# First projection of a hybrid encoder layer: finished blocks in two 512-column buffers, six weight quadrants held, loads into the buffer freed last

## Chip, cores and metric

The kernel runs on one core of a Trainium2 chip. The metric is the device time of one execution in microseconds (us). Before the change three runs gave 2162.06, 2162.21 and 2162.73 us; their median is 2162.21 us. Engines are named as the profile names them: PE multiplies matrices, PEld loads its weights, ACT and DVE work on whole tiles, POOL and SP here mostly issue DMA transfers.

## What is computed

One encoder layer over 512 tokens of width 2048, in float32:

```
h = rmsnorm(x, attn_norm_w)
proj = h @ w_in
aq, ak, av, gq, gk, gv, gr, glr = split(proj)
...
x = x + concat([attn_out, gla_out]) @ w_out
h = rmsnorm(x, ffn_norm_w)
x = x + (silu(h @ w_gate) * (h @ w_up)) @ w_down
return rmsnorm(x, final_norm_w)
```

The change lies in `proj = h @ w_in`, in those 4096 columns of it that are called gr, gq, gk, aq and ak.

## The kernel before

**Units and steps.** The class `Front` computes these columns in 16 units of 256 columns by 512 tokens: four of gr, four of gq and gk, eight of aq and ak. A unit is a two-by-two block product done with seven products instead of eight: weights and activations are both cut into quadrants, sums of quadrants are formed on DVE, and seven products are added up in accumulators of PSUM called X, V, Y, W and Z. One product is a *step*, numbered n = 0 to 6 in its unit (and i over all 112). `Feed` computes w_gate and w_up with the same step code (both inherit from `Units`).

**What one step costs.** Every float32 operand is split into a high and a low part. ACT casts the weight quadrant to the high part (`cast`, L1563), DVE subtracts to get the low part (`sub`, L1569), and DVE adds quadrants where the product wants a sum (`add`, L1538). PE then does eight matmuls of 128 x 512 with the high part (L1601) and eight of 128 x 256 with the low part (L1604).

**Order of the work.** `Front.run` goes over the steps. In loop step i it first asks for weight loads (`fetch`, issued by SP, L1531), then emits cast, add and sub of step i + 2 (`lead`), then empties what step i - 1 left in PSUM (`evac_`), and last emits the matmuls of step i. Each engine works through its own part in this order. Where a step reads an accumulator that `evac_` has to read first, PE waits: product 6 adds to W, which the add at L1645 (emptying step 4) reads.

**Emptying.** After n = 0, 1 and 2 ACT copies accumulators (L1629, L1632, L1636) and DVE subtracts (L1638). After n = 3, 5 and 6 ACT copies (L1623) and DVE adds (L1624) a quarter of the finished block; after n = 4 DVE adds at L1645 and L1647. Then `finish` scales the block on DVE (L1801, or L1799 for two units) and POOL writes it to DRAM (L1802).

**Buffers.** `s4` is a pool of 33 buffers of 128 x 1024, named b0 to b32; `s2` has 36 of 128 x 512, named a0 to a35. `get` takes the buffer that has been free longest, `put` appends one at the end. A buffer is put back when the program has emitted its last reader, which may be well before that reader runs: whoever gets the buffer waits for it. Weight quadrants, sums of quadrants, high parts, low parts and the finished block all come from `s4`. `fetch` holds up to eight quadrants and leaves at least three buffers free (`KEEP`). `sub` puts its source back, `products` the high and low part, and `finish` the finished block, whose last reader is the write to DRAM.

Quadrant tiles are 128 x 8 x 128, 512 KB. The following lines show the mechanism:

```
s.i = self.free.popleft()
...
hi, lo = self.his.pop(i), s4.get(F32R, [P, NP, P])
...
if n == 3:
    self.outs[u] = s4.get(F32, [P, 2, 512])
    out("X", 0)
```

Of the kernel before, what the change touches and what calls it, by code (L numbers as in the profile page):

```python
# [19 lines left out]
OP = mybir.AluOpType  # L20
# [94 lines left out]
def put(*slots):  # L115
    for s in slots:
        if s.home is not None:
            s.home.free.append(s.i)


def layer(nc, tc, x, attn_norm_w, w_in, rel_table, gw_f, gb_f, gw_b, gb_b, gla_norm_w, w_out,
# [7 lines left out]
    with tc.manual_schedule(), \  # L129
# [1381 lines left out]
        class Units:  # L1511

            ORDER = ("B11", "T1", "T2", "B21", "T3", "B22", "T4")
            FREES = {0: "B11", 4: "T3", 5: "B22", 6: "T4"}
            AHEAD, KEEP = 2, 3

            def open(self, first):
                self.steps = [(u, n) for u in range(first, len(self.units)) for n in range(7)]
# [5 lines left out]
            def fetch(self, most=8):  # L1524
                while self.todo and len(self.quads) < most and len(s4.free) > self.KEEP:
                    u, b = self.todo.popleft()
                    r = self.quads[u, b] = s4.get(F32, [P, NP, P])
                    w, col = self.place(u)
                    k, h = divmod(b, 2)
                    rows = w[:, col + h * P:col + (h + 1) * P].rearrange("(q k p) c -> k p q c", k=2, p=P)  # L1530
                    sp.dma_start(out=r.t, in_=rows[k])  # L1531
# [77 lines left out]
            def evac_late(self):  # L1609
                late, self.late_ = self.late_, []  # L1610
                for i in late:
                    self.evac_(i)

            def evac_(self, i):

                u, n = self.steps[i]
                B = lambda k: self.banks[u, k]
                a, z = slice(0, 256), slice(256, 512)
                tt = dve.tensor_tensor

                def out(k, c):
                    o = self.outs[u].t.rearrange("p f t -> p (f t)")[:, c * 256:(c + 1) * 256]
                    act.copy(o, B(k).t[:, a])  # L1623
                    tt(o, o, B(k).t[:, z], op=OP.add)  # L1624
                    put(self.banks.pop((u, k)))

                if n == 0:
                    b = self.banks[u, "Y"] = self.seat(i + 1)
                    act.activation(b.t, B("X").t, AF.Copy, scale=-1.0)  # L1629
                if n == 1:  # L1630
                    y = self.parts[u] = s2.get()
                    act.copy(y.t, B("V").t)  # L1632
                    put(self.banks.pop((u, "V")))
                if n == 2:
                    b = self.banks[u, "W"] = self.seat(i + 1)
                    act.activation(b.t, B("Y").t, AF.Copy, scale=-1.0)  # L1636
                    b = self.banks[u, "Z"] = self.seat(i + 1)
                    tt(b.t, self.parts[u].t, B("Y").t, op=OP.subtract)  # L1638
                    put(self.banks.pop((u, "Y")))
                if n == 3:  # L1640
                    self.outs[u] = s4.get(F32, [P, 2, 512])
                    out("X", 0)
                if n == 4:
                    y = self.parts.pop(u)
                    tt(y.t, y.t, B("W").t, op=OP.add)  # L1645
                    o = self.outs[u].t.rearrange("p f t -> p (f t)")
                    tt(o[:, 768:1024], y.t[:, a], y.t[:, z], op=OP.add)  # L1647
                    put(y)
                if n == 5:
                    out("Z", 1)  # L1650
                if n == 6:
                    out("W", 2)
                    c_ = self.outs.pop(u)
                    urgent.append(self.finish(u, c_, c_.t.rearrange("p f t -> p (f t)")))

        class Feed(Blocks, Units):

# [40 lines left out]
            def evac(self, u, banks):  # L1698


                a, z = slice(0, 256), slice(256, 512)
                w, j = self.units[u]
                add = lambda o, x_, y_: dve.tensor_tensor(o, x_, y_, op=OP.add)
                c_ = s4.get(F32, [P, 2, 512])
                c = c_.t.rearrange("p f t -> p (f t)")
                A, B, C, E = (b.t for b in banks)
                t1, t2 = s2.get(), s2.get()
                act.copy(t1.t[:, a], A[:, a])
                add(c[:, a], A[:, z], t1.t[:, a])
# [11 lines left out]
                yield from self.finish(u, c_, c)  # L1721
                yield

            def finish(self, u, c_, c):
                w, j = self.units[u]
                if w is w_gate:
                    dve.tensor_tensor(c_.t, c_.t, rb[2].t[:, None, :].to_broadcast([P, 2, 512]), op=OP.mult)
                    yield
                    tables(SILU)
                    for f in range(2):  # L1730
                        act.activation(c_.t[:, f], c_.t[:, f], AF.Silu, scale=1.0 - 2.0 * f)
                    self.gate = c_
                else:
                    dve.tensor_tensor(c_.t, c_.t, self.gate.t, op=OP.mult)
                    put(self.gate)
                    pool.dma_start(out=gd[j], in_=c)
                    put(c_)

            def run(self):
# [42 lines left out]

        class Front(Units):

            def __init__(self):
                self.units = [(w_in, C_GR + g * 256) for g in range(4)] + [(w_in, C_GQ), (w_in, C_GK)] + \
                    [(w_in, C_GQ + 256), (w_in, C_GK + 256)] + \
                    [(w_in, c + g * 256) for g in range(4) for c in (C_AQ, C_AK)]
                self.xs = xi
                self.open(0)  # L1790
# [1 line left out]
            def place(self, u):  # L1792
                return self.units[u]

            def finish(self, u, c_, c):
                def do():
                    r = rb[1].t[:, None, :].to_broadcast([P, 2, 512])
                    if u in (4, 6):
                        dve.scalar_tensor_tensor(c_.t, c_.t, P ** -0.5, r, op0=OP.mult, op1=OP.mult)  # L1799
                    else:  # L1800
                        dve.tensor_tensor(c_.t, c_.t, r, op=OP.mult)  # L1801
                    pool.dma_start(out=grd[u] if u < 4 else gfd[u - 4] if u < 8 else qkd[u - 8], in_=c)  # L1802
# [571 lines left out]
```

## Time and profile before

| what | value |
|---|---|
| median of three runs | 2162.21 us |
| the profiled execution, its own time | 2165.34 us |
| its span in the trace | 2163.6 us |
| PE busy | 2135.8 us (99%), 11418 matmuls |
| DVE busy | 1724.6 us (80%) |
| ACT busy | 1229.1 us (57%) |
| steps of `Front` in the trace | 106.3 us to 441.8 us |
| steps of `Feed` in the trace | about 896 us to 1718 us |

The profiled execution took 3.1 us more than the median of the runs; its own time is 1.7 us more than its span. A view called *waits* names, for each group of instructions, whom it waited for, the total in us, the number of times and the longest. In a *timeline* a row has its start, its length, the engine, the line and the operation, merged over a few instructions (x8), and in brackets how long the engine had been idle before it and who ended that. In a table *by windows* each engine has its busy time in that stretch, and PEclk is the granted TensorE clock. Lengths of matmuls overlap, so a step's length is best read from starts.

### The profile page before, as it was taken

To read this page: it belongs to the slowest core of one execution; us is meant where nothing else is said; L and a number is where in the kernel's file an instruction comes from. 1 tells how busy PE (TensorE), PEld (TensorE's weight loads), DVE (VectorE), ACT (ScalarE), POOL (GpSimd) and SP (SyncE) were. 2 spreads that over 40 slices of the span, in tenths; PEclk is the share of its full clock that TensorE was granted. 3 is DMA by queue.
4 is the path that set the end of the run, shared out by engine and by line. 5 is a ranking of instruction groups with operands and counts; after the bars stand their busy time and mean duration, and the time that the engine had idled before them with its cause. 6 is when DMAs were issued, how large, how long until landed. Compare 5 with 4: busy or idle time off the path is not lost.

```text
span 2163.6 us, 30507 instructions
## 1 busy us (share of the span) xinstructions
PE 2135.8 (99%) x11418; PEld 1835.3 (85%) x11418; DVE 1724.6 (80%) x2345; ACT 1229.1 (57%) x2051; POOL 172.6 (8%) x278
## 2 busy tenths in 40 slices
PE   9999999999999999999999999999999999999998
PEld 7887888888888888988888888888888888888887
DVE  5677787868877657988888888888888878897885
ACT  7444444457786545555545555555555576666762
POOL 0000000112312000000000000000000020232000
PEclk9999999999999999999999999999999999999999
DMA  6543444365754423444434334443344497899572
GB/s 203 172 149 108 136 120 134 105 199 171 201 199 140 134 98 117 137 127 123 116 113 136 116 118 117 127 132 112 114 130 117 173 241 248 200 256 241 194 256 78
DMA packets 340594, 330.47 MB, mean 153 GB/s; under 512 B 15133, under 2 KB 260365, under 8 KB 340446
## 3 DMA queue, kind: packets, MB, share of 16 engines
q1 hardware_dynamic: 313598, 258.07, 39.1%
q0 software_dynamic: 26528, 69.91, 12.5%
q8 instruction: 90, 1.47, 0.3%
q14 instruction: 58, 0.48, 0.1%
q10 hardware_dynamic: 320, 0.53, 0.1%
HBM read 267.55 MB, written 60.92 MB: 152 GB/s over the span
## 4 chain that ended last, share of the span: by engine, by line
PE 83%; issue 13%; DMA 1%; DVE 1%; ACT 1%; POOL 0%; DVEq 0%; SPq 0%; POOLq 0%; ACTq 0%
PE ps L1601 26%; PE ps L1604 14%; PE ps L349 6%; PE ps L350 6%; PE ps L348 6%; PE ps L2057 5%; PE ps L2056 5%; PE ps L2055 5%; PE ps L699 1%; PE ps L2270 1%; PE ps L2272 1%; PE ps L2271 1%; PE ps L643 1%; PE ps L724 1%; PE ps L723 1%
## 5 line engine op out<-in xcount | busy, mean ns | idle before, releaser
L1569 DVE TENSOR_TENSOR b<-b,b 128x1024 fp32r<-128x1024 f32 x406 | 495.2, 1220 | 133.9 <-ACT b L1563 122.0
L1563 ACT CAST b<-b 128x1024 fp32r<-128x1024 f32 x406 | 425.9, 1050 | 200.7 <-DVE b L1569 92.0
L1601 PE MATMUL ps<-a,b 128*128 128x512 f32 x1656 | 427.0, 393 | 16.4 <-DVE a L1645 11.1
L1601 PE MATMUL ps<-b,b 128*128 128x512 f32 x1592 | 421.2, 393 | 0.5 <-ACT ps L1629 0.5
L1601 PEld LDWEIGHTS ps<-a,b 128*128 128x128 f32 x1656 | 304.8, 189 | 81.9 <-issue 13.2
L1601 PEld LDWEIGHTS ps<-b,b 128*128 128x128 f32 x1592 | 280.2, 189 | 43.2 <-ACT ps L1629 0.7
L1538 DVE TENSOR_TENSOR b<-b,b 128x1024 f32<-128x1024 f32 x232 | 282.6, 1218 | 1.3 <-PE ps L350 0.7
L1604 PEld LDWEIGHTS ps<-b,b 128*128 128x128 f32 x1592 | 232.6, 190 | 23.4
L1604 PE MATMUL ps<-a,b 128*128 128x256 f32 x1656 | 242.9, 283 | 0.0
L1604 PE MATMUL ps<-b,b 128*128 128x256 f32 x1592 | 242.8, 282 | 0.0
L1604 PEld LDWEIGHTS ps<-a,b 128*128 128x128 f32 x1656 | 225.2, 192 | 8.5
L1623 ACT COPY b<-ps 128x256 f32<-128x256 f32 x174 | 64.6, 371 | 223.5 <-PE ps L1604 223.5
L2031 DVE TENSOR_TENSOR b<-b,b 128x1024 fp32r<-128x1024 f32 x112 | 136.5, 1220 | 34.8 <-ACT b L2023 34.8
L348 PE MATMUL ps<-b,b 128*128 128x512 f32 x344 | 139.8, 407 | 0.0
L350 PE MATMUL ps<-b,b 128*128 128x512 f32 x344 | 135.1, 393 | 0.0
L349 PE MATMUL ps<-b,b 128*128 128x512 f32 x344 | 134.9, 392 | 0.0
L2023 ACT CAST b<-b 128x1024 fp32r<-128x1024 f32 x112 | 116.6, 1052 | 26.6 <-DVE b L2011 15.3
L220 DVE TENSOR_TENSOR b<-b,b 128x512 fp32r<-128x512 f32 x120 | 79.5, 683 | 26.7 <-ACT b L239 26.5
L1624 DVE TENSOR_TENSOR b<-b,ps 128x256 f32<-128x256 f32 x174 | 72.2, 415 | 27.7 <-ACT b L1623 27.7
L2055 PE MATMUL ps<-b,a 128*128 128x512 f32 x240 | 93.4, 389 | 0.0
L2056 PE MATMUL ps<-b,a 128*128 128x512 f32 x240 | 93.4, 389 | 0.0
L2057 PE MATMUL ps<-b,a 128*128 128x512 f32 x240 | 93.4, 389 | 0.0
(308 smaller groups left out, 3580.6 us busy)
## 6 DMA issues: line engine op xcount, KB each, us to landing
b<-in_w_in_dram SPq DMA_DIRECT2D x94, 512.0 KB, 4.1
b<-in_w_gate_dram SPq DMA_DIRECT2D x88, 512.0 KB, 4.4
b<-in_w_up_dram SPq DMA_DIRECT2D x88, 512.0 KB, 3.8
b<-in_w_down_dram SPq DMA_DIRECT2D x88, 512.0 KB, 6.9
b<-in_w_out_dram SPq DMA_DIRECT2D x32, 512.0 KB, 4.4
md<-a POOLq DMA_DIRECT2D x56, 256.0 KB, 6.8
gd<-b POOLq DMA_DIRECT2D x22, 512.0 KB, 5.3
b<-gd SPq DMA_DIRECT2D x22, 512.0 KB, 5.5
```

What stands on the lines that cost most here:

```text
L348: mm(o, xh.t[:, c], wh.t[:, w], start=first and not on, stop=False, skip_group_check=on)
L349: mm(o, xh.t[:, c], wl.t[:, w], start=False, stop=False, skip_group_check=on)
L350: mm(o, xl.t[:, c], wh.t[:, w], start=False, stop=last, skip_group_check=on)
L1538: tt = lambda o, x_, y_: dve.tensor_tensor(o.t, x_.t, y_.t, op=OP.add)
L1563: act.copy(hi.t, home[key].t)
L1569: dve.tensor_tensor(lo.t, home[key].t, hi.f, op=OP.subtract)
L1601: mm(o.rearrange("p (s t) -> p s t", s=2), hi.t[:, q], self.xs[q][self.ORDER[n]], start=new and q == 0, stop=False, skip_group_check=True)
L1604: mm(o[:, 0:256], lo.t[:, q], self.xs[q][self.ORDER[n]][:, 0], start=False, stop=q == NP - 1, skip_group_check=True)
L2031: dve.tensor_tensor(lo.t, s.t, hi.f, op=OP.subtract)
L2055: mm(o, xh[:, t], wh, start=new and j == 0, stop=False, skip_group_check=True)
L2056: mm(o, xh[:, t], wl, start=False, stop=False, skip_group_check=True)
L2057: mm(o, xl[:, t], wh, start=False, stop=last and j == 1, skip_group_check=True)
```

## The change

Four things change, all in this one stage; one of them touches code that `Feed` uses too, without effect there.

- The finished block of `Front` is held in two `s2` buffers of 128 x 512 (`home`, `block`) instead of one `s4` buffer.
- `finish` therefore scales it with two instructions of 128 x 512 and writes it with two transfers of 256 KB.
- `Front` holds six weight quadrants instead of eight: `fetch(6)`. The loads asked for before the stage begins still go up to eight.
- In `Front` a load takes the `s4` buffer that was put back last, instead of the one free longest (`NEWEST`, a rotation of the list of free buffers). All others still take the oldest.

```
@@ class Units
+            NEWEST = False
             def fetch(self, most=8):
                 while self.todo and len(self.quads) < most and len(s4.free) > self.KEEP:
                     u, b = self.todo.popleft()
+                    if self.NEWEST:
+                        s4.free.rotate(1)
                     r = self.quads[u, b] = s4.get(F32, [P, NP, P])
...
+            def home(self):
+                return s4.get(F32, [P, 2, 512])
+
+            def block(self, u, c):
+                return self.outs[u].t.rearrange("p f t -> p (f t)")[:, c * 256:(c + 1) * 256]
...
                 if n == 3:
-                    self.outs[u] = s4.get(F32, [P, 2, 512])
+                    self.outs[u] = self.home()
                     out("X", 0)
@@ class Front(Units)
+            NEWEST = True
+
+            def home(self):
+                return s2.get(), s2.get()
+
+            def block(self, u, c):
+                f, h = divmod(c, 2)
+                return self.outs[u][f].t[:, h * 256:(h + 1) * 256]
+
-            def finish(self, u, c_, c):
+            def finish(self, u, c_):
                 def do():
-                    r = rb[1].t[:, None, :].to_broadcast([P, 2, 512])
-                    if u in (4, 6):
-                        dve.scalar_tensor_tensor(c_.t, c_.t, P ** -0.5, r, op0=OP.mult, op1=OP.mult)
-                    else:
-                        dve.tensor_tensor(c_.t, c_.t, r, op=OP.mult)
-                    pool.dma_start(out=grd[u] if u < 4 else gfd[u - 4] if u < 8 else qkd[u - 8], in_=c)
-                    put(c_)
+                    d = grd[u] if u < 4 else gfd[u - 4] if u < 8 else qkd[u - 8]
+                    for f, o in enumerate(c_):
+                        if u in (4, 6):
+                            dve.scalar_tensor_tensor(o.t, o.t, P ** -0.5, rb[1].t, op0=OP.mult, op1=OP.mult)
+                        else:
+                            dve.tensor_tensor(o.t, o.t, rb[1].t, op=OP.mult)
+                        pool.dma_start(out=d[:, f * 512:(f + 1) * 512], in_=o.t)
+                    put(*c_)
...
                 for i, (u, n) in enumerate(self.steps):
-                    self.fetch()
+                    self.fetch(6)
                     self.lead(i + self.AHEAD)
```

PE's instructions stay in the same order. What moves is which buffer each of the others gets. In the rows below a tile's name begins with its buffer: b32_239 is a tile in buffer b32, the number behind it only counts tiles. All are from the end of unit 5 and the beginning of unit 6.

ACT before, from the last quarter of unit 5's block (b32_227, which is later scaled and written to DRAM) to the fourth cast after it:

```order
L1623 COPY b32_227_2064<-ps3_61_2038 128x256
L1563 CAST b16_237_2159<-b30_209_1931 128x1024
L1629 ACTIVATE ps6_64_2163<-ps5_63_2138 128x512
L1563 CAST b32_239_2182<-b18_199_1855 128x1024
L1632 COPY a8_66_2187<-ps7_65_2165 128x512
L1563 CAST b18_243_2209<-b5_232_2110 128x1024
L1636 ACTIVATE ps0_66_2213<-ps6_64_2163 128x512
L1563 CAST b8_245_2233<-b26_194_1807 128x1024
```

The second cast goes into b32, the buffer of the block that is just being written to DRAM, and the third into b18, the very buffer that the second has read. ACT at the same place after the change:

```order
L1632 COPY a9_77_2076<-ps3_61_2049 128x256
L1566 CAST b19_229_2173<-b9_213_2041 128x1024
L1638 ACTIVATE ps6_64_2177<-ps5_63_2152 128x512
L1566 CAST b28_231_2196<-b14_200_1917 128x1024
L1641 COPY a10_78_2201<-ps7_65_2179 128x512
L1566 CAST b29_235_2223<-b6_225_2124 128x1024
L1645 ACTIVATE ps0_66_2227<-ps6_64_2177 128x512
L1566 CAST b30_237_2247<-b10_194_1865 128x1024
```

The block is in a8 and a9, and none of the four casts goes into a buffer named in the rows before it.

DVE before, at the same place: the last quarter of the block, its scaling (L1801), and the subs of the next casts:

```order
L1569 TENSOR_TENSOR b8_235_2134<-b5_232_2110,b9_234_2132 128x1024
L1624 TENSOR_TENSOR b32_227_2064<-b32_227_2064,ps3_61_2038 128x256
L1801 TENSOR_TENSOR b32_227_2064<-b32_227_2064,a28_45_650 128x1024
L1569 TENSOR_TENSOR b6_238_2161<-b30_209_1931,b16_237_2159 128x1024
L1538 TENSOR_TENSOR b5_232_2110<-b5_232_2110,b30_209_1931 128x1024
L1569 TENSOR_TENSOR b19_240_2185<-b18_199_1855,b32_239_2182 128x1024
```

DVE there after the change, where the scaling is L1819:

```order
L1572 TENSOR_TENSOR b17_228_2148<-b6_225_2124,b12_227_2146 128x1024
L1633 TENSOR_TENSOR a9_77_2076<-a9_77_2076,ps3_61_2049 128x256
L1819 TENSOR_TENSOR a8_76_2075<-a8_76_2075,a28_45_650 128x512
L1819 TENSOR_TENSOR a9_77_2076<-a9_77_2076,a28_45_650 128x512
L1572 TENSOR_TENSOR b26_230_2175<-b9_213_2041,b19_229_2173 128x1024
L1541 TENSOR_TENSOR b6_225_2124<-b6_225_2124,b9_213_2041 128x1024
L1572 TENSOR_TENSOR b22_232_2199<-b14_200_1917,b28_231_2196 128x1024
```

One instruction has become two, at the same place in the row; everything else stands as it stood, with other buffers.

SP before, the four quadrants of unit 6 and the first of unit 7:

```order
L1531 DMA b26_194_1807<-in_w_in_dram 128x8x128
L1531 DMA b18_199_1855<-in_w_in_dram 128x8x128
L1531 DMA b19_200_1857<-in_w_in_dram 128x8x128
L1531 DMA b30_209_1931<-in_w_in_dram 128x8x128
L1531 DMA b17_215_1982<-in_w_in_dram 128x8x128
```

SP after, the same five loads:

```order
L1534 DMA b10_194_1865<-in_w_in_dram 128x8x128
L1534 DMA b14_200_1917<-in_w_in_dram 128x8x128
L1534 DMA b12_203_1942<-in_w_in_dram 128x8x128
L1534 DMA b9_213_2041<-in_w_in_dram 128x8x128
L1534 DMA b32_214_2043<-in_w_in_dram 128x8x128
```

The loads stand in the same order, but each is asked for later in the program: the fourth of unit 6 at loop step n = 3 of unit 5, where it stood at n = 6 of unit 4 before; the fifth in the same loop step as the fourth, where it stood at n = 1 of unit 5. Their buffers, b9 and b32, are those of the low and the high part of unit 5's product n = 2, the product that PE does just before.

More of the change, by code (lines that the diff above doesn't have):

```diff
@@ L1621, in out @@
                 def out(k, c):
-                    o = self.outs[u].t.rearrange("p f t -> p (f t)")[:, c * 256:(c + 1) * 256]
+                    o = self.block(u, c)
                     act.copy(o, B(k).t[:, a])
@@ L1645, in evac_ @@
                     tt(y.t, y.t, B("W").t, op=OP.add)
-                    o = self.outs[u].t.rearrange("p f t -> p (f t)")
-                    tt(o[:, 768:1024], y.t[:, a], y.t[:, z], op=OP.add)
+                    tt(self.block(u, 3), y.t[:, a], y.t[:, z], op=OP.add)
                     put(y)
@@ L1735, in finish @@
                     put(self.gate)
-                    pool.dma_start(out=gd[j], in_=c)
+                    pool.dma_start(out=gd[j], in_=c_.t.rearrange("p f t -> p (f t)"))
                     put(c_)
```

6 lines of the change are left out of this document (3 added, 3 removed).

## The prediction

> **What bounds the kernel now.** I read the page first: PE fills 99% of the span. So only what shortens or opens PE's pauses counts, and the next question is where they are. The table by windows answers that (columns PE, PEld, DVE, ACT, POOL, then PEclk):
>
> ```profile
> PE 2135.8 (99%) x11418; PEld 1835.3 (85%) x11418; DVE 1724.6 (80%) x2345; ACT 1229.1 (57%) x2051; POOL 172.6 (8%) x278
> ...
> 200.00:300.00 100.00, 94.13 (x532) 81.84 (x531) 78.54 (x86) 46.11 (x63) 2.12 (x4) 1.00 0.44 122
> 300.00:400.00 100.00, 94.98 (x540) 82.72 (x539) 79.54 (x87) 45.83 (x62) 2.66 (x5) 1.00 0.46 132
> 1000.00:1400.00 400.00, 400.00 (x2292) 351.98 (x2291) 340.40 (x368) 209.28 (x289) 5.31 (x10) 1.00 0.42 122
> ```
>
> In `Front` PE stands still for over 5 us in each 100. In `Feed` (1000 to 1400), with the same step code, it never does, although DVE has more to do there (85% against 79%). So `Front` does not lack engine time; it waits in the wrong places. PE's own waits, whole program:
>
> ```profile
> PE ps L1601 <- DVE a L1645: 11.1, 12, 1.1
> PE ps L1601 <- ACT ps L1629: 4.0, 2, 3.5
> PE ps L1601 <- ACT ps L1636: 1.7, 2, 1.4
> ```
>
> Twelve times, once per unit, product 6 waits for the add at L1645. The third row is two more waits in these units. Next I read the timeline at one such wait, the one that ends unit 6; POOL's row is the write of unit 5's block, on which the chain begins:
>
> ```profile
> 240.56 0.53 POOL L1802 DMA_DIRECT2D gfd<-b  x1 [20.09 <-DVE b L1801]
> 243.53 1.05 ACT L1563 CAST b<-b 128x1024 fp32r<-128x1024 f32 x1 [3.33 <-DMA gfd<-b]
> 244.61 1.22 DVE L1569 TENSOR_TENSOR b<-b,b 128x1024 fp32r<-128x1024 f32 x1 [2.07 <-ACT b L1563]
> 245.87 1.05 ACT L1563 CAST b<-b 128x1024 fp32r<-128x1024 f32 x1 [0.81 <-DVE b L1569]
> 246.95 1.23 DVE L1569 TENSOR_TENSOR b<-b,b 128x1024 fp32r<-128x1024 f32 x1 [1.12 <-ACT b L1563]
> ...
> 250.59 2.00 PE L1601 MATMUL ps<-b,b 128*128 128x512 f32 x8
> 253.57 0.68 DVE L1645 TENSOR_TENSOR a<-a,ps 128x512 f32<-128x512 f32 x1
> 254.39 0.93 PE L1601 MATMUL ps<-a,b 128*128 128x512 f32 x3 [0.85 <-DVE a L1645]
> ```
>
> ACT stands still for 3.33 us because its cast got the buffer of the block that is still on its way to DRAM. Behind that cast on ACT are the emptying copies and the next casts; DVE's subs wait for the casts (2.07), the next cast for a sub (0.81, it got that sub's source buffer), the next sub for that cast (1.12). DVE has lost 3.19 us and from 246.95 on works without a pause until L1645 at 253.57. PE started product 5 at 250.59, so it had finished product 4, which L1645 reads, about then; DVE was simply late. The waits of the whole stage have the same members:
>
> ```profile
> ACT b L1563 <- DVE b L1569: 92.0, 56, 2.4
> DVE b L1569 <- ACT b L1563: 55.2, 41, 4.0
> ACT b L1563 <- DMA qkd<-b: 17.7, 5, 4.1
> ACT b L1563 <- DMA grd<-b: 14.6, 4, 5.2
> ACT b L1563 <- DMA gfd<-b: 13.3, 4, 3.3
> ```
>
> Thirteen casts wait for a write, for 17.7 + 14.6 + 13.3 = 45.6 us, and 56 casts for a sub.
>
> **What a unit costs without this.** The stage holds its own experiment: unit 14 has no loads left to ask for, so more buffers are free. Rows of PE: the start of units 2, 14 and 15. Rows of DVE: L1645 in unit 14, and a sub that still waits for a write.
>
> ```profile
> 151.64 2.00 PE L1601 MATMUL ps<-b,b 128*128 128x512 f32 x8
> 402.74 2.00 PE L1601 MATMUL ps<-b,b 128*128 128x512 f32 x8
> 422.30 2.00 PE L1601 MATMUL ps<-b,b 128*128 128x512 f32 x8
> ...
> 409.71 2.36 DVE L1569 TENSOR_TENSOR b<-b,b 128x1024 fp32r<-128x1024 f32 x2 [1.03 <-DMA qkd<-b]
> 417.48 0.68 DVE L1645 TENSOR_TENSOR a<-a,ps 128x512 f32<-128x512 f32 x1
> 419.50 2.00 PE L1601 MATMUL ps<-a,b 128*128 128x512 f32 x8
> ```
>
> Unit 14 takes 422.30 - 402.74 = 19.56 us, 2.79 us a step, with L1645 done at 418.16 and product 6 starting without a wait at 419.50: 1.3 us to spare. Units 2 to 13 take 402.74 - 151.64 = 251.10 us. At 19.56 each they would take 234.72. **The excess is 16.4 us.** Of it 11.1 + 1.7 = 12.8 us stands in the rows of waits; the other 3.6 us, 0.26 for each of the 14 waits, is PE getting back into its pace.
>
> **The change, part by part.**
>
> *The block leaves `s4`, and loads take the newest buffer.* Together they let the list of free buffers age. Followed through the program, in the steady part of the stage every cast, sub and add gets a buffer whose last reader belongs to loop step i - 2 or earlier, where before it was often the product, the sub or the write just ahead. That is the pattern that `Feed` has too, where PE did not pause in 400 us. The write's wait leaves ACT altogether; the next tile in an output buffer comes at least eight steps later, 8 x 2.79 = 22 us. So DVE gets back the 3.19 us of the timeline, and L1645 must only be about 1.1 us earlier (0.85 of pause and the 0.26). What is late next: nothing I can find; the spare time is then that of unit 14. I take the whole 16.4 us off. If only the waits at L1645 go and the two at L1636 stay, it is 16.4 - 1.7 - 2 x 0.26 = 14.2.
>
> *Two scalings instead of one.* A 128 x 1024 scaling against a 128 x 512 one from two `s2` tiles, the nearest there is:
>
> ```profile
> L1801 DVE TENSOR_TENSOR b<-b,a 128x1024 f32<-128x1024 f32 x14 | 17.1, 1225 | 0.5
> L1042 DVE TENSOR_TENSOR a<-a,a 128x512 f32<-128x512 f32 x16 | 10.2, 684 | 1.7 <-ACT a L1034 1.7
> ```
>
> 2 x 684 - 1225 = 143 ns a unit, 16 x 0.143 = 2.3 us on DVE. It lies beside PE: the 1.3 us ahead of product 6 cover it, so 0; without that cover 2.3 us. The Trainium skill speaks against this edit: VectorE: DVE Perf Modes, section "TRN2 errata — SBUF-src ops pay a fixed extra latency per instruction", says that many small tiles pay a fixed time each that one large tile pays once. By its measured 151 cycles at 0.96 GHz I estimate 157 ns for each extra instruction, 2.5 us in all if nothing hid it; the two rows above agree closely, so the sum would be the same.
>
> *Two writes of 256 KB instead of one of 512.* Columns: count, size, median us from issue to landing.
>
> ```profile
> qkd<-b POOLq DMA_DIRECT2D x8, 512.0 KB, 3.0
> xd<-b POOLq DMA_DIRECT2D x16, 256.0 KB, 2.7
> b<-md SPq DMA_DIRECT2D x13, 512.0 KB, 10.0
> ```
>
> POOL has idled for 20 us before each write and waits for the landing of none, so a second issue of 0.53 us costs 0. One thing is queued behind them: at the end of the stage POOL's first reads for the attention go into tiles that unit 14's block has left, so POOL waits for that landing, about 3 us, with the other reads behind it. They serve work beside the next projection, which PE goes through without them; I take 0, and 3 us if that cover is gone.
>
> *Six quadrants, loads later.* The shortest way from load to use is the fourth quadrant: asked for at loop step n = 3, when PE has finished product 2, first read by a cast that ACT can do four steps later. That leaves 4 x 2.79 = 11.2 us. All loads of the stage landed within 4.6 us of their issue:
>
> ```profile
> L1531 SPq DMA_DIRECT2D b<-in_w_in_dram x55: 367/368/780, 112.3 to 396.1; - x55
> ...
> DMA to landing us min/median/max: 3.9/4.1/4.6
> ```
>
> Two asked for together, as the fourth and fifth are, were among these. SP's queue holds nothing else here, so a load that waits for PE delays only later loads. Cost 0.
>
> *What stays.* At the start of the stage PE waits 3.5 us for the copy at L1629, and the step after it is slow:
>
> ```profile
> 115.77 3.30 PE L1601 MATMUL ps<-a,b 128*128 128x512 f32 x8 [3.51 <-ACT ps L1629]
> ...
> 120.69 2.00 PE L1601 MATMUL ps<-b,b 128*128 128x512 f32 x8
> ```
>
> The casts there wait for writes of an earlier job, whose buffers are handed out as before. I leave it; if it went too, it would bring at most 3.5 us and the 1.3 by which this row's step is longer than its neighbour: 4.8 us.
>
> **The sum.** The profiled execution would take 2165.34 - 16.4 = 2148.9 us (span 2163.6 - 16.4 = 2147.2). The runs' median lies 3.1 us lower: 2162.21 - 16.4 = **2145.8 us**. PE is the chain to the end, so what it gains here arrives there.
>
> **The rivals.** About 0.2%, 4.3 us, is what a measurement of this kernel can tell from no change.
>
> *Part of it comes back* (9%). L1645 is still late in some units, through the extra DVE time (2.3 us), the reads behind unit 14's write (3) or the waits at L1636 (2.2). All three together leave 16.4 - 7.5 = 8.9 us: 2153.3. Against it speaks the cover of each, above.
>
> *DVE is late by itself* (6%). L1645 stands behind a row of subs and adds, and if their sheer length set it, 3 us returned to ACT would only move the pause. Then the time is 2162.2. For it: DVE works without a pause from 246.95 to L1645. Against it: unit 14, and `Feed`, where DVE is busier and PE does not wait.
>
> *Loads come too late* (3%): slower. One mechanism: SP may only start a load when PE has finished the product just before, and if landing takes longer than 11.2 us, ACT waits at the fourth quadrant of all 16 units. It decides from (16.4 + 4.3) / 16 = 1.3 us beyond that, 12.5 us; at 13 us the stage loses 16 x 1.8 = 28.8, net 12.4: 2174.6. For it: loads now follow PE closely and fall together with the writes. Against it: even the slowest median of a transfer this size in the table, 10.0 us, would fit, and here the longest was 4.6.
>
> *The start goes too* (2%): 16.4 + 4.8 = 21.2, 2141.0.
>
> My forecast has the remaining 80%. The range: upward the split scalings and the delayed reads, 2.3 + 3 = 5.3, and a little of the waits at L1636, to 2152; downward about half of the start, to 2143. Left out are parts of the partial case and the three others. Faster: 80 + 9 + 2 = 91%; same 6%; slower 3%.
>
> **What would show it.** Right: in the waits of the changed kernel the rows PE <- L1645 (then L1654) and ACT cast <- DMA grd, gfd, qkd are gone from units 2 to 13, casts wait for PE's results as ACT runs ahead, a unit takes 19.6 us from start to start, and PE fills 100 us in 100 from 200 to 400. The start's 3.5 us is still there. Wrong: the casts or adds of the stage wait for DMA in_w_in (loads late); L1654 is still waited for with no write in the chain (DVE itself); or the stage gains its 16 us and a later stage shows new pauses of PE.

## The result, and the profile after

The changed kernel takes 2146.45 us (median of four runs, 2145.25 to 2147.80), the kernel before 2162.14 us beside it. The ratio is 0.9929, 95% interval 0.9911 to 0.9946: faster by 15.7 us, which is only 0.7% but lies outside the noise. The prediction said 2145.8. The profiled execution of the changed kernel took 2146.47 us with a span of 2144.7. Of the four executions of the kernel e6 below, one ran at a granted clock of 0.556 and took 3553.04 us; e6's median is that of the other three.

**Where the time came from.** The stage runs from PE's first product of `Front` to the first matmul of line 348 behind it. First the two rows of the timeline of before, then those of after (before, line 1604 was 1601; the other lines moved by 3 to 18, so L1645 is now L1654, L1563 is L1566, L1569 is L1572, L1801 is L1819):

```profile
106.31 1.98 PE L1601 MATMUL ps<-b,b 128*128 128x512 f32 x8
...
441.85 0.40 PE L348 MATMUL ps<-b,b 128*128 128x512 f32 x1
```

```profile
104.19 1.98 PE L1604 MATMUL ps<-b,b 128*128 128x512 f32 x8
...
423.02 0.40 PE L348 MATMUL ps<-b,b 128*128 128x512 f32 x1
```

The stage took 441.85 - 106.31 = 335.54 us and now takes 423.02 - 104.19 = 318.83: **16.7 us less**, where 16.4 had been forecast. What follows the stage takes as long as before, within 0.1 us (2163.6 - 441.85 against 2144.7 - 423.02). The spans differ by 18.9, for the stage also begins 2.1 us earlier. That is not the change: a kernel below whose program ahead of the stage is that of before (six held in the stage, nothing else) starts it at 104.23. The profiled execution of before was a long one, 3.2 us above its median: 2.1 of these lie ahead of the stage, and up to 1.1 may lie in it. So effects are compared by the length of the stage, and the medians stand beside it.

Units 2 to 13, in which the prediction had found the excess, begin and end with these rows of the changed kernel:

```profile
149.28 2.00 PE L1604 MATMUL ps<-b,b 128*128 128x512 f32 x8
...
383.92 2.00 PE L1604 MATMUL ps<-b,b 128*128 128x512 f32 x8
```

They take 383.92 - 149.28 = 234.64 us, 19.55 each, where they took 251.10: 16.5 of the 16.7 us lie there.

**The pauses are gone.** The table by windows of the changed kernel, columns PE, PEld, DVE, ACT, POOL, PEclk, and all waits of PE over 1.1 us in total from its page of waits:

```profile
200.00:300.00 100.00, 100.00 (x575) 88.00 (x573) 85.58 (x99) 49.69 (x68) 5.40 (x10) 1.00 0.49 138
300.00:400.00 100.00, 100.00 (x574) 87.93 (x573) 85.54 (x99) 47.67 (x65) 5.39 (x10) 1.00 0.45 127
```

```profile
PE ps L1604 <- ACT ps L1638: 3.8, 2, 3.3
PE ps L1102 <- DMA b<-gvd: 1.2, 2, 0.9
```

PE fills 100 us in 100 where it filled 94 to 95, and DVE is busier per us than before because the same work is done in less time. The row of the twelve waits at L1645 has no successor at L1654. The waits of the other engines in the stage (100 to 430 us) include:

```profile
ACT a L1632 <- PE ps L1607: 97.1, 48, 5.2
...
DVE b L1572 <- ACT b L1566: 25.8, 18, 1.7
```

ACT now waits for PE's results, 97.1 us in one row alone: it runs ahead. In the whole stage no cast waits for the write of one of its blocks (45.6 us before). The timeline of the changed kernel at the same place as the prediction's, the end of unit 6:

```profile
228.44 1.29 DVE L1819 TENSOR_TENSOR a<-a,a 128x512 f32<-128x512 f32 x2
229.41 1.14 POOL L1820 DMA_DIRECT2D gfd<-a  x2 [18.41 <-DVE a L1819]
...
233.76 1.06 ACT L1566 CAST b<-b 128x1024 fp32r<-128x1024 f32 x1
...
242.22 0.68 DVE L1654 TENSOR_TENSOR a<-a,ps 128x512 f32<-128x512 f32 x1
...
244.25 2.00 PE L1604 MATMUL ps<-a,b 128*128 128x512 f32 x8
248.97 1.14 POOL L1820 DMA_DIRECT2D gfd<-a  x2 [18.41 <-DVE a L1817]
```

The add at L1654 ends at 242.90, product 6 starts at 244.25 without waiting: 1.35 us to spare. The two writes come again after 248.97 - 229.41 = 19.56 us, the length of a unit that was read off unit 14.

### The profile page after: what moved, and what is told of

Same layout as the page of the kernel before. It is cut to its first block, busy times and chain, and to the rows that moved or that the text cites. A ratio compares the mean times of both kernels' runs of the same rounds, so it can differ in the third digit from the quotient of the medians.

```text
span 2144.7 us, 30564 instructions
## 1 busy us (share of the span) xinstructions
PE 2129.7 (99%) x11418; PEld 1832.4 (85%) x11418; DVE 1725.8 (80%) x2361; ACT 1228.4 (57%) x2051; POOL 181.4 (8%) x294
## 4 chain that ended last, share of the span: by engine, by line
PE 95%; DMA 1%; issue 1%; DVE 1%; ACT 1%; POOL 0%; SPq 0%; DVEq 0%; POOLq 0%; ACTq 0%
PE ps L1604 35%; PE ps L1607 18%; PE ps L350 6%; PE ps L349 6%; PE ps L348 6%; PE ps L2073 5%; PE ps L2074 5%; PE ps L2075 5%; PE ps L699 1%; PE ps L643 1%; PE ps L2288 1%; PE ps L2289 1%; PE ps L2290 1%; PE ps L644 1%; PE ps L723 1%
## 5 line engine op out<-in xcount | busy, mean ns | idle before, releaser
L1572 DVE TENSOR_TENSOR b<-b,b 128x1024 fp32r<-128x1024 f32 x406 | 495.6, 1221 | 94.8 <-ACT b L1566 92.4
L1566 ACT CAST b<-b 128x1024 fp32r<-128x1024 f32 x406 | 425.2, 1052 | 63.3 <-PE ps L1607 27.8
L1604 PE MATMUL ps<-a,b 128*128 128x512 f32 x1656 | 425.9, 393 | 3.3 <-ACT ps L1638 3.3
L1632 ACT COPY b<-ps 128x256 f32<-128x256 f32 x126 | 46.9, 372 | 206.3 <-PE ps L1607 206.3
L348 PE MATMUL ps<-a,b 128*128 128x512 f32 x216 | 86.6, 401 | 0.0
```

What stands on the lines that cost most here:

```text
L348: mm(o, xh.t[:, c], wh.t[:, w], start=first and not on, stop=False, skip_group_check=on)
L1566: act.copy(hi.t, home[key].t)
L1572: dve.tensor_tensor(lo.t, home[key].t, hi.f, op=OP.subtract)
L1604: mm(o.rearrange("p (s t) -> p s t", s=2), hi.t[:, q], self.xs[q][self.ORDER[n]], start=new and q == 0, stop=False, skip_group_check=True)
```

## The experiments

Two readings were to be told apart. **The write theory:** all that costs is that a cast on ACT gets the buffer of a block on its way to DRAM; whatever moves that write's wait off ACT brings the 16 us. **The rival,** which the prediction's words come near ("together they let the list age"): the short hand-ons from a sub to the next cast (56 waits, 92 us before) are part of it, so that only loads into the newest buffers and the block elsewhere, together, bring it. Then the sizes of two margins were tested, DVE's 1.35 us and the lead of the loads, and last what the start of the stage is worth. All results (each ratio goes by runs of the kernel before on the same chip; the stage is that of the profiled execution):

| kernel | median, us | ratio to before, 95% | stage, us |
|---|---|---|---|
| before | 2162.14 | | 335.54 |
| changed | 2146.45 | 0.9929 [0.9911, 0.9946] | 318.83 |
| e1 block in `s2` only | 2148.16 | 0.9935 [0.9918, 0.9951] | 319.14 |
| e2 newest buffer only | 2147.41 | 0.9929 [0.9914, 0.9943] | 320.09 |
| e3 six held only | 2146.89 | 0.9926 [0.9911, 0.9941] | 318.85 |
| e4 changed, eight held | 2147.64 | 0.9932 [0.9917, 0.9947] | 318.87 |
| e5 e3 with the write back on ACT | 2171.61 | 1.0044 [1.0029, 1.0059] | 344.30 |
| e6 changed, one more DVE add a unit | 2146.48 | 0.9927 [0.9910, 0.9944] | 318.85 |
| e7 changed, three more | 2160.77 | 0.999 [0.998, 1.000] | 333.69 |
| e8 changed, five held | 2146.52 | 0.9927 [0.9912, 0.9941] | 318.84 |
| e9 changed, six first loads | 2141.66 | 0.9904 [0.9888, 0.9921] | 314.07 |
| e10 e9, first loads into the oldest | 2142.13 | 0.9907 [0.9893, 0.9922] | 314.08 |
| e11 changed, four held | 2176.72 | 1.0067 [1.0052, 1.0082] | 347.82 |
| e12 before, six held at both places | 2142.84 | 0.9907 [0.9891, 0.9924] | 314.51 |

**e1, the block in `s2` alone.** Against the changed kernel:

```
@@ class Front
-            NEWEST = True
...
-                    self.fetch(6)
+                    self.fetch(8)
```

> Only the finished block moves, into two 512-column buffers; eight quadrants are held and loads take the oldest buffer, as before. Casts get no buffer of a write any more, but 32 of 56 of them in the steady part still get the source of the sub just ahead, and every sub gets a buffer of the product just done. Theory WRITE (the block's write, met by a cast, is what makes DVE late; the rest of the tight handing on is harmless): the whole gain, about 2146 us, no wait of PE for the add at L1645, a unit at 19.6 us. Theory AGE (a cast tied to the sub just ahead is enough to make DVE late): only a small part, 2156 to 2162 us, and PE still waits there in most units.

Measured: 2148.16 us, the stage 319.14. The list of free buffers does not age here, and the casts still follow subs closely (waits from 125 to 400 us):

```profile
ACT b L1566 <- DVE b L1572: 39.7, 39, 1.6
```

39 such waits (54 before, in the same stretch), yet none of PE for L1654. The short hand-on from sub to cast costs nothing as long as no write stands ahead of it.

**e2, only the newest buffer for a load.** Against the kernel before:

```
@@ class Units, fetch
+                    if self.NEWEST:
+                        s4.free.rotate(1)
@@ class Front
+            NEWEST = True
```

> Only loads take the buffer freed last; the block stays in a 1024-column buffer and eight quadrants are held. The block's buffer now goes to a load in the very loop step in which its write is issued, so SP waits for the write instead of ACT; 16 of 56 casts and 8 of 56 subs still get the buffer of the sub just ahead, 48 subs that of the product just done. Loads are asked for 8 to 10 loop steps ahead of use. WRITE: whole gain, about 2146 us. AGE: half or less, 2154 to 2160 us.

Measured: 2147.41 us, the stage 320.09. That is 1.3 us more than the changed kernel's, and all of it lies in the first unit (130.83 - 104.27 = 26.56 us against 129.50 - 104.19 = 25.31), where the granted clock stayed low longer, as the last section shows. The block is in `s4` again and its write still makes somebody wait. The waits of SP's queue, 125 to 400 us:

```profile
SPq L1534 <- DMA qkd<-b: 40.4, 5, 8.6
SPq L1534 <- DMA grd<-b: 32.6, 4, 9.0
SPq L1534 <- DMA gfd<-b: 31.8, 4, 8.0
```

A load now gets the block's buffer, and SP waits for the write 13 times, up to 9.0 us. SP has nothing else to do and its load is wanted much later. The wait is longer than ACT's was, and costs nothing.

**e3, only six quadrants.** Against the kernel before, one number:

```
-                    self.fetch()
+                    self.fetch(6)
```

> Only six quadrants are held; the block stays in a 1024-column buffer and loads take the oldest one. The two buffers that this frees age the list: every cast gets a buffer that was freed two loop steps earlier, and the block's buffer goes to a load two steps after its write was issued. 24 of 56 subs still get a buffer of the sub just ahead, which is on DVE itself. WRITE and AGE both: the whole gain, about 2146 us. If it is short of it (2150 us or more), something else in the change is needed that neither theory names.

Measured: 2146.89 us, the stage 318.85, as the whole change. SP's waits for the same writes are longer still:

```profile
SPq L1534 <- DMA qkd<-b: 69.1, 6, 11.8
SPq L1534 <- DMA grd<-b: 46.9, 4, 12.5
SPq L1534 <- DMA gfd<-b: 45.8, 4, 11.4
```

With more buffers free, the block's buffer reaches the head of the list where a load is next, not a cast.

**e4, the change with eight quadrants.** Against the changed kernel: `fetch(6)` becomes `fetch(8)`.

> The block in two 512-column buffers and loads into the buffer freed last, but eight quadrants held. No cast meets a write; 8 of 56 casts and 16 of 56 subs get the buffer of the sub just ahead, 40 subs that of the product just done. WRITE: whole gain, about 2146 us. AGE: something between, 2148 to 2156 us, fewer casts waiting for a sub than with the block moved alone, and accordingly fewer waits of PE.

Measured: 2147.64 us, the stage 318.87. Once the block is out of the way, the number of quadrants held adds nothing.

**e5, the write put back on ACT.** e3, with one buffer moved by hand: the cast of product 4 gets the buffer that was last written to DRAM.

```
@@ e3, lead
+                    if i % 7 == 4 and self.written in s4.free:
+                        s4.free.remove(self.written)
+                        s4.free.appendleft(self.written)
@@ e3, finish
+                    self.written = c_.i
```

> Six quadrants held and nothing else of the change, as in the third kernel, but the cast of product 4 is made to take the buffer of the block whose write was issued just before, as in the kernel before; all other casts keep buffers freed two steps earlier. So the meeting of cast and write is put back alone. Theory WRITE (that meeting costs the time by itself): 8 to 16 us come back, 2155 to 2162 us, PE waits for the add at L1645 in most units. Theory BOTH (it costs only where casts and subs also hand buffers on so tightly that DVE cannot catch up; with older buffers ACT runs ahead, the write is issued earlier against the cast, the wait shrinks to some 1.5 us and DVE's free 3 us a unit take it): nothing comes back, 2146 to 2148 us, casts wait for writes 13 times, about 20 us in all, PE never.

Measured: 2171.61 us, the stage 344.30, 25.5 us longer than e3's. Waits of ACT's casts and of PE from 125 to 400 us (its lines stand four further down than the changed kernel's at these places):

```profile
ACT b L1570 <- DMA qkd<-b: 27.3, 5, 6.1
ACT b L1570 <- DMA gfd<-b: 21.0, 4, 5.3
...
ACT b L1570 <- DMA grd<-b: 14.0, 4, 5.4
...
PE ps L1608 <- DVE a L1658: 9.7, 9, 1.1
...
PE ps L1608 <- ACT ps L1649: 6.4, 10, 1.3
```

The timeline of one unit (L1658 is the add that was L1645):

```profile
236.69 0.53 POOL L1815 DMA_DIRECT2D gfd<-b  x1 [21.16 <-DVE b L1814]
...
242.43 1.05 ACT L1570 CAST b<-b 128x1024 fp32r<-128x1024 f32 x1 [5.23 <-DMA gfd<-b]
243.52 1.23 DVE L1576 TENSOR_TENSOR b<-b,b 128x1024 fp32r<-128x1024 f32 x1 [4.85 <-ACT b L1570]
...
251.56 0.68 DVE L1658 TENSOR_TENSOR a<-a,ps 128x512 f32<-128x512 f32 x1
...
252.39 1.85 PE L1608 MATMUL ps<-a,b 128*128 128x512 f32 x7 [1.07 <-DVE a L1658]
```

From unit 4 on it is the prediction's chain again: write, cast, sub, add, PE. In most units PE also waits for the copy at L1649, which stands behind the late cast on ACT. But the size fits neither forecast (8 to 16 us, or none), and the wait is not the old one: ACT stands still for 5.2 us, not 3.3. The block's write goes out here within 0.1 us of a load (236.69, the load 236.61) and lands after 5.7 us:

```profile
gfd<-b POOLq DMA_DIRECT2D x4, 512.0 KB, 5.7
```

In the kernel before the next load went out 1.84 us after the write (242.40 and 240.56), and the median for the same row was 2.9.

In units 2 and 3 of e5 the wait is still about as long as in the kernel before. These are the starts of units 2, 3 and 4, and the casts that wait in between:

```profile
150.86 2.00 PE L1608 MATMUL ps<-b,b 128*128 128x512 f32 x8
...
157.30 1.05 ACT L1570 CAST b<-b 128x1024 fp32r<-128x1024 f32 x1 [2.86 <-DMA grd<-b]
...
170.41 2.00 PE L1608 MATMUL ps<-b,b 128*128 128x512 f32 x8
...
177.33 1.05 ACT L1570 CAST b<-b 128x1024 fp32r<-128x1024 f32 x1 [3.34 <-DMA grd<-b]
...
190.13 2.00 PE L1608 MATMUL ps<-b,b 128*128 128x512 f32 x8
```

Unit 2 takes 19.55 us, as in the changed kernel, and unit 3 takes 19.72, only 0.17 more. In the kernel before, unit 2 had a wait of 3.32 us and took 172.26 - 151.64 = 20.62, 1.07 more. So a wait of the old length costs little by itself. What e5 lacks is the close hand-on: from 125 to 400 us no cast of e5 waits for a sub's buffer, where 54 did before. With it ACT and DVE did not catch up. In unit 1 a cast waited 2.19 us before and 2.40 in e5, and both units took 19.78 us, as in the changed kernel; but the next block's write went out 155.52 - 151.64 = 3.88 us after its unit began before (3.04 in unit 1), and 2.58 in e5, as in unit 1.

So the write theory holds in this: without the write's wait on ACT nothing is lost (three unlike ways, e1 to e3, each bring 15 to 17 us of stage), and a wait of 5.2 us costs some 2 us a unit by itself. The strict rival, that only an aged list brings the gain, falls with e1. But the pauses of the kernel before, with waits of 3.3 us, needed both, the write's wait and the close hand-ons, which is what theory BOTH says. This last part rests on two units of one trace.

**e6 and e7, DVE's margin.** The changed kernel with one add of 128 x 512 on a spare buffer ahead of L1654 in each unit (e6), or three (e7). This is added work, and nothing reads it.

```
@@ ahead of the add at L1654
+                        for _ in range(1):
+                            tt(self.spare.t, rb[1].t, rb[1].t, op=OP.add)
```

> The changed kernel with one more DVE instruction of 128 x 512 on a spare buffer just ahead of the add at L1654 in each of the 16 units, about 0.6 us each, 10 us of DVE in all. In the trace of the changed kernel that add ends 1.35 us before product 6 needs it. Theory SPARE (1.35 us of DVE time a unit are free there): no change, within 2 us of 2146.5. Theory DVE (DVE sets the pace of the stage after the change, so the split scalings show too): 8 to 10 us more, 2155 us.

Measured: 2146.48 us, the stage 318.85: nothing.

> The same with three such instructions a unit, 1.8 to 2.0 us each unit. SPARE: 0.5 to 0.7 us more than the free 1.35, with 0.26 for PE's recovery 0.8 to 1 us in about 15 units: 12 to 15 us more, about 2160 us, and PE waits for L1654 again in nearly every unit. DVE: 16 x 1.9 = 30 us more, 2177 us.

Measured: 2160.77 us, the stage 333.69, 14.9 us more than the changed kernel. PE's waits in e7:

```profile
PE ps L1604 <- DVE a L1657: 9.7, 14, 0.7
```

Three adds are 3 x 0.68 = 2.05 us, the margin was 1.35, and PE waits 9.7 / 14 = 0.69 us a unit, as the subtraction has it. The margin is real, and once it is used up each wait costs more than its own length: a unit now takes 20.49 us, 0.94 more than 19.55. Fourteen of these make 13.2 us; the rest lies in unit 0 (131.91 - 104.81 = 27.10 us against 25.31), where the granted clock stayed low longer (last section).

**e8 and e11, the lead of the loads.** The changed kernel with `fetch(5)` and with `fetch(4)`.

> The changed kernel with five quadrants held instead of six. The second of a unit's quadrants that are added in place is then asked for only two loop steps before its cast and add, which stand just ahead of the add at L1654 on ACT and DVE. Landing took 5.3 us in the median and 6.4 at most, ACT and DVE run about one step ahead of PE, so they wait 1 to 3 us for it in each unit. If loads matter as the prediction had it (only the time left between request and use counts): DVE waits for DMA of w_in about 14 times, PE 0 to 1 us in each unit, 2147 to 2158 us. If loads are hidden anyway: 2146.5 us and no such waits.

Measured: 2146.52 us, the stage 318.84. The waits from 125 to 400 us show the loads arriving late for ACT and DVE for the first time, and no wait of PE. The waits came as the first forecast had them, only shorter, and the time as the second:

```profile
ACT b L1566 <- DMA b<-in_w_in_dram: 15.8, 14, 1.3
DVE b L1541 <- DMA b<-in_w_in_dram: 4.3, 13, 0.5
```

> The changed kernel with four quadrants held in the stage instead of six: the first quadrant of a unit is then asked for about one loop step ahead of its cast, 2.8 us, against a landing of 4.0 to 5.3 us. LEAD theory (a load is hidden as long as its lead is over its landing time, which held at five and six): the cast and the add behind it are 2 to 3 us late in each unit, more than the 1.35 us that DVE has to spare, and PE waits 1 to 2 us a unit and loses its pace: 2165 to 2195. Rival (ACT's and DVE's own head start of several steps swallows it): 2146.5.

Measured: 2176.72 us, slower than the kernel before; the stage 347.82, 29.0 us longer than the changed kernel's. Its waits from 125 to 400 us:

```profile
DVE b L1541 <- DMA b<-in_w_in_dram: 35.3, 12, 3.3
ACT b L1566 <- DMA b<-in_w_in_dram: 34.2, 12, 3.8
...
PE ps L1604 <- DVE a L1654: 20.3, 12, 2.1
```

The two loads waited for go out together, for example at 225.26 and 225.72. DVE's add starts on the first at 229.77 and ACT's cast on the second at 231.35, 4.5 and 5.6 us later, so the loads were no slower than pairs are elsewhere (last section). They were asked for about one loop step ahead, 2.8 us, and DVE's add of quadrants waits some 3 us in each unit. That is more than the margin of 1.35, and L1654 is late by 2.1 us at most. The prediction's slower rival is a mechanism of this kernel, then, but its place is four quadrants, not six: between them ACT and DVE took up the lateness of e8.

**e9 and e10, the start of the stage.** The prediction left 3.5 us of pause and a slow step of 1.3 there and priced the two at 4.8 together. In the changed kernel both are still to be seen:

```profile
111.84 1.04 ACT L1566 CAST b<-b 128x1024 fp32r<-128x1024 f32 x1 [2.21 <-DMA vd<-b]
112.79 0.58 ACT L1638 ACTIVATE ps<-ps 128x512 f32<-128x512 f32 x1
...
113.43 3.51 PE L1604 MATMUL ps<-a,b 128*128 128x512 f32 x8 [3.29 <-ACT ps L1638]
```

It is the same figure: a cast waits for a write (here of the job before, to vd), the emptying copy stands behind it on ACT, and PE waits for the copy. e9 asks for six quadrants ahead of the stage instead of eight, which leaves two more old buffers for the first casts:

```
@@ before_front
-                fr.fetch()
+                fr.fetch(6)
```

> The changed kernel, with one number more: the loads asked for ahead of the stage go up to six quadrants instead of eight. START theory (the 3.5 us pause of PE at the stage's start has the same cause as the pauses removed: ACT's cast of step 2 meets the write of the job before, 2.2 us late, and the emptying copy behind it is late for PE): with two buffers less taken by first loads, the first casts get buffers that are no longer being written, the pause of 3.3 us and the slow step behind it go, about 4 to 5 us less, some 2141.5 to 2142.5. Rival (the pause is set by something else, the copy itself or products of the job before, or the casts meet those writes anyway): no change, 2146.5. A third: the two loads asked for later are late at the first unit, and PE waits there instead: above 2146.5.

Measured: 2141.66 us, 4.8 less than the changed kernel; the stage 314.07, also 4.8 less. Its timeline at the same step:

```profile
110.14 0.58 ACT L1638 ACTIVATE ps<-ps 128x512 f32<-128x512 f32 x1
...
110.78 2.11 PE L1604 MATMUL ps<-a,b 128*128 128x512 f32 x8
```

The copy starts 2.7 us earlier (110.14, where it was 112.79), PE has no wait left in the whole stage, and these matmuls take 2.11 us. Casts here do still wait for vd, but 1.1 us, and behind the copy.

e10 is e9 with the first loads in the oldest buffers (`NEWEST` is set only when the stage begins). The change had given them buffers that put DVE's add and ACT's cast 12 and 14.9 us behind a load, in the job ahead of the stage. These are e9's waits from 80 to 105 us:

```profile
ACT b L1566 <- DMA b<-in_w_in_dram: 14.9, 1, 14.9
DVE b L1541 <- DMA b<-in_w_in_dram: 12.5, 2, 12.0
```

> As the run with six first loads, and the first loads take the oldest buffer as before; the newest is taken only inside the stage. START theory: the same 2141.5 to 2142.5, and DVE's 12 us wait for the first loads, which the change had brought and for which PE did not wait, is gone. If that wait cost something unseen, this one is faster than the run with six first loads by up to 1 us; if the two are equal within 0.5 us, it cost nothing.

Measured: 2142.13 us, the stage 314.08. Those rows are gone and the time is the same, so the long waits, which the prediction did not have, cost nothing.

**e12, the least that does it.** The kernel before with six quadrants at both places, and nothing else:

```
@@ before_front
-                fr.fetch()
+                fr.fetch(6)
@@ Front.run
-                    self.fetch()
+                    self.fetch(6)
```

> The kernel before with one number changed in two places: six quadrants held, ahead of the stage and in it; the block, its scaling, its write and the order of the free buffers as before. WRITE theory (all that matters is that no cast of ACT meets a write, at the start or in the units): the same as the changed kernel with six first loads, 2141.5 to 2142.5, stage 314.1 us, SP waiting for writes with its loads instead. Rival (the two causes are not independent, or the larger block in the 1024-column pool costs something at the start): 2143.5 to 2147.

Measured: 2142.84 us, the stage 314.51. The median falls between the two forecasts (2141.5 to 2142.5, and 2143.5 to 2147); its interval of the ratio, 0.9891 to 0.9924, is that of e9 within 0.0003, and the stage is 0.44 us longer than e9's. So one number in two places gives all but that of what any kernel here gave: its stage is 4.3 us shorter than the changed kernel's, its median 3.6 us lower.

## Why the prediction was right, point by point

- **The bound and the excess.** Right. PE's pauses were what could be had, and unit 14 gave their price: 16.4 us forecast, 16.7 measured in the stage. Units 2 to 13 gave 16.5 of it. The 12.8 us in rows of waits alone would have been too little; the 3.6 us of recovery were real (last section). By medians the gain is 15.7, with the interval about 12 to 19 us.
- **The chain from the write to PE.** Right in its members, which e5 shows again. The prediction puts the late DVE down to the write's wait and to the hand-ons behind it (2.07, 0.81 and 1.12 in its timeline) without weighing them. Units 2 and 3 of e5 show that a wait of 2.9 to 3.3 us without the hand-ons costs 0.17 us at most.
- **Why the change removes it.** Here a step was worded too widely: "together they let the list of free buffers age" makes the ageing the cause and the parts depend on each other. The runs showed that each of the three parts alone brings the gain (e1 to e3) and that ageing isn't needed (e1), though it is not idle either: with an old list, e5's first waits cost next to nothing. The sentence behind it, "the write's wait leaves ACT altogether", is the one that carries the number. The sum did not suffer, since it took the whole excess once.
- **Two scalings, at 0.** Right. They take 1.29 us together against 1.22 for the single one, 0.07 and not 0.143 more: here two in a row cost less than twice the single one of 0.684 us. The Trainium skill's fixed extra time per instruction (VectorE: DVE Perf Modes, section "TRN2 errata — SBUF-src ops pay a fixed extra latency per instruction"), from which 157 ns had been estimated, does not appear in full in this pair; the trace decides. Up to 0.68 us more was free anyway (e6).
- **Two writes, at 0.** Right. POOL's issues take 1.14 us instead of 0.53 in each unit, and POOL idles for 18.4 us before them. The reads behind unit 14's write, bounded at 3 us, did not wait for its landing; POOL waited for PE there, for 2.17 us, and PE for none of them.
- **Later loads, at 0.** The term was right, its input was not. The landing line covers only the loads whose landing the trace tells, 20 of 55. In the kernel before all 20 had gone out alone; none of its 13 pairs was among them, as the prediction took it. In the changed kernel the 20 are loads of pairs, and they landed in 4.0 to 6.4 us, median 5.3, not within 4.6.

```profile
DMA to landing us min/median/max: 4.0/5.3/6.4
```

  The lead of 11.2 us covered that too. e8 and e11 place the edge, between five quadrants and four.
- **The start stays.** Right, and its price of 4.8 us was what e9 got. The buffers there were not quite "handed out as before": the first loads took others, which gave the waits of 12 and 14.9 us that e10 removes, at no cost.
- **The rivals.** No part of the gain came back, DVE was not late by itself (e6, e7), and loads were in time.

## What to carry to other kernels

When an engine waits for a buffer, ask which engine could wait instead at no cost: here the same write delayed SP by up to 12.5 us for nothing, and ACT by 3.5 us a unit (45.6 / 13) at 16 us of the stage's time, because DVE's subs wait for ACT's casts, and the add that PE needs stands behind those subs. How much such a wait costs depends on whether the engines behind it can catch up: 3.3 us cost 1.1 us a unit where casts and subs handed buffers on closely, and 0.17 where they did not. A stretch of the trace that happens to lack the fault (unit 14) prices it better than the sum of its waits does. And try each part of such a change alone: the least of them, a smaller number of prefetched tiles, did all of it, and the same number in a second place brought over 4 us more.

## What was not expected of the hardware

- **A pause of 3.3 us slows the matmuls behind it, one of 1 us does not.** The table by windows of the changed kernel around the start (columns as above, the granted clock third from the end), then of e9, then of e7:

```profile
113.00:118.00 5.00, 4.57 (x17) 3.85 (x18) 4.62 (x4) 2.86 (x4) 0.00 (x0) 0.66 0.00 0
118.00:123.00 5.00, 5.00 (x28) 4.27 (x27) 4.00 (x5) 3.22 (x5) 0.00 (x0) 1.00 0.01 2
```

```profile
113.00:118.00 5.00, 5.00 (x31) 4.41 (x30) 4.83 (x5) 3.58 (x6) 0.00 (x0) 1.00 0.60 159
```

```profile
113.00:118.00 5.00, 3.94 (x10) 3.21 (x11) 4.45 (x4) 3.49 (x5) 0.00 (x0) 0.51 0.00 0
118.00:123.00 5.00, 5.00 (x27) 4.51 (x26) 2.56 (x4) 1.54 (x2) 0.00 (x0) 0.80 0.00 0
```

  In the changed kernel the granted clock is 0.66 in the 5 us behind the pause and back at 1.00 in the next; in finer windows it is 0.50 from 113.8 to 117.1 and 1.00 from 117.3 on. Without the pause it stays at 1.00. In e7, behind a pause of the same length, it stays low longer, and in e2 too (0.50 and 0.83), and their first units are longer, by 1.3 us in e2; a difference of that size between two stages can be this alone. The Trainium skill (TensorE: Matmul & The Clock Gate, section "Part 1: The HAM clock gate (the "warmup" mystery)") says that the clock halves after at least one idle window of about 3.4 us and comes back after a busy one of about that length. The low stretch of the changed kernel agrees with it in length; the pause does not quite, for it lasts 3.29 us. In e11 the clock fell once even behind a pause of 1.79 us (257.05; it is 0.50 from 258.4 to 261.6), while twelve other pauses of 1.5 to 2.1 us there left it at 1.00. So the measured pauses are shorter than the stated window.
- **A short pause costs a quarter of a microsecond beyond its length, at full clock.** The pauses of the kernel before left the clock at 1.00 in every window from 200 to 400. In the steady pace a product's first matmul starts 0.16 us before the recorded end of the one ahead, as at 244.25 in the changed kernel (243.30 + 1.11 = 244.41); behind a pause this overlap is lost. And the first eight matmuls then take 2.08 us (at 254.39 before) instead of 2.00. Together that is 0.24 us at each of the twelve waits for L1645, the prediction's 0.26, and e7's units show the same: 0.94 more for a wait of 0.69.
- **The second of two loads that go out together lands later.** In the changed kernel 13 pairs of loads go out, mostly 0.47 us apart. The seven first loads whose landing the trace tells landed in 4.0 to 4.5 us, the thirteen second ones in 5.0 to 6.4 (for example 4.5 us for the load at 255.62, 5.8 for the one at 256.09). Loads that went out alone in the kernel before took 3.9 to 4.6. This explains why the landing line has a median of 5.3 to 5.4 us in kernels that hold six (the changed one, e3, e12) and 4.0 to 4.2 in those that hold eight, five or four: it counts other loads. It does not show that a load lands later where six are held. In e5 the blocks' writes that go out beside a load land later too, 5.7 us against 2.9; how the transfers delay each other was not tested.
